# Attention probabilities transposed by VectorE in 32 by 32 blocks instead of by TensorE

## The chip, the cores and the metric

The kernel runs on one core of one Trainium2 chip. The metric is device time in microseconds (us) of one execution. The kernel before takes 2535.78 us, the median of 3 runs (2535.55 to 2538.28).

## The reference

One layer of a hybrid encoder in fp32 for 2048 tokens of 1024 features. The input projection gives, per token, 512 columns q and 128 columns each of k and v for a sliding-window attention (8 query heads and 2 key heads of 64), and 4 x 512 columns for a gated linear recurrence (HGRN2). The two outputs are put side by side, projected and added to the input; a cross attention into 256 memory tokens and a SwiGLU block follow. The part that the change touches is the sliding-window attention:

```python
s = jnp.einsum('bnqhgd,bnkhd->bnhgqk', qc, kband) * (Dh ** -0.5)
s = jnp.where(valid, s, NEG_INF)
p = jax.nn.softmax(jnp.concatenate([s, sink], axis=-1), axis=-1)[..., :L]
o = jnp.einsum('bnhgqk,bnkhd->bnqhgd', p, vband)
```

Scores `s` come with queries on the rows. The product with `v` sums over keys, so on the chip the probabilities `p` must be turned: keys on the partitions.

## The kernel before, in words

Every fp32 product is made of products of a high and a low half (`hi`, `lo`: the rounded value and what rounding left over), so TensorE does two or three matmuls for each.

**Stages.** (1) `in_first` makes the input projection of the first 1024 tokens (to about 275 us of the span). (2) A mixed stretch follows, to about 604 us: the attention `swa` for 16 tiles of 128 tokens ("pairs" n = 0 to 15, each with the tile before it as keys), the recurrence `hgrn` for tiles 0 to 7, and the input projection of the other 1024 tokens, `in_proj`, whose columns (`in_cols`, matmul lines L156 to L158) are dealt out between the pairs and give TensorE long runs of matmuls that wait for nothing of the attention. (3) The rest: tiles 8 to 15 of `hgrn`, the folding of the cross-attention weights, and then the large products (L1162 to L1164), which take about three quarters of the time.

**One pair.** `swa_front` loads q and k from DRAM (`z_d`) twice over both halves of the partitions, and makes the low halves on VectorE and ScalarE (L787, L788 for q, L1001, L1002 for k); TensorE makes the scores (L822, L823, into PSUM), VectorE masks them and takes the minimum (L827), ScalarE the exponential with its sum (L831), GpSimd adds the sink's share (L834, L837), VectorE takes the reciprocal and scales (L839, L842). `swa_back`, called one pair later, turns the probabilities on TensorE in squares of 128 (L856, 16 for each pair, 8 for the first), makes halves out of PSUM (L860 on ScalarE, L861 on VectorE), multiplies with v (L865, L866), adds the two halves (L869, L870) and stores 256 KB (`y_d<-ys`, L78).

**What sets the order.** The Tile framework's scheduler orders the instructions once, when the program is built; each engine then works off its own list in that order, and a waiting instruction holds up all that stand behind it on its engine. DMAs are issued by SyncE (SP), from one list too (L75 loads, L78 stores), a few by GpSimd. In the program's list each of SP's DMAs waits for one of eight semaphores in turn, which the DMA eight places ahead of it sets when it lands.

Of the kernel before, what the change touches and what calls it, by code (L numbers as in the profile page):

```python
# [48 lines left out]
class Layer:  # L49
# [111 lines left out]
    def run(self):  # L161
# [4 lines left out]
        self.z_d = tc.dram_tile([DIN, T], F32, name="z_d")  # L166

# [26 lines left out]
    def mix(self):  # L194
        tc, I = self.tc, self.I
        kw = dict(reuse_waits="tile")
        with contextlib.ExitStack() as left:
# [5 lines left out]
            with (  # L203
                tc.tile_pool(name="t1", bufs=3, **kw) as self.ts,
                tc.tile_pool(name="t2", bufs=3, **kw) as self.tb,
                tc.tile_pool(name="s1", bufs=2, side="right", **kw) as self.st_pool,
                contextlib.ExitStack() as at,
            ):
                self.banks(at, "ps1", **MOST)
                self.raws = 3  # L210
                u = self.in_first()
# [52 lines left out]
            with (  # L264
# [6 lines left out]
                self.raws = 4  # L271
# [164 lines left out]
    def pair_tile(self):  # L436
        self._n += 1
        return self.st_pool.tile([P, 2, D], F32, tag="pair", name=f"pair_{self._n}", bufs=5)
# [27 lines left out]
    def in_first(self):  # L466
# [154 lines left out]
        z = self.pair_tile()  # L621
        for s in range(2):
            for i in range(2):
# [3 lines left out]
                nc.scalar.activation(z[:, i, s * 512:(s + 1) * 512], ps, AF.Copy)  # L627
        for i in range(2):
            self.store(self.z_d[c0 + i * P:c0 + (i + 1) * P, TB:2 * TB], z[:, i, :])
        return u  # L630

    def in_block(self, ca, cb, x, ahead, beside, get, plain, between):
# [16 lines left out]
        def out(i, j, a, b):  # L649
            c0 = (ca, cb)[i] * P  # L650
            if plain:
                self._n += 1
                t = self.st_pool.tile([P, 512], F32, tag="part", name=f"zp_{self._n}", bufs=3)
                nc.scalar.activation(t, a, AF.Copy)
                self.store(self.z_d[c0:c0 + P, j * 512:(j + 1) * 512], t)
                return
            if not z:
                z.append(self.pair_tile())
            zs = z[0][:, i, j * 512:(j + 1) * 512]
# [10 lines left out]
            else:  # L670
                self._n += 1
                t = self.st_pool.tile([P, 512], F32, tag="part", name=f"th_{self._n}", bufs=3)
# [3 lines left out]
        def after():  # L676
# [14 lines left out]
            for i, c in enumerate(() if plain else (ca, cb)):  # L691
                self.store(self.z_d[c * P:(c + 1) * P, 0:TB], z[0][:, i, :])
# [16 lines left out]
    def in_cols(self, b, u, cols, e1):  # L709
# [5 lines left out]
        for s in range(TB // 512):  # L715
            sl = slice(s * 512, (s + 1) * 512)
            for i, c in enumerate(cols):
# [4 lines left out]
                if c0 < C_QH or C_IH <= c0 < C_GH:  # L722
# [11 lines left out]
        for i, c in enumerate(cols):  # L734
# [5 lines left out]
            self.store(self.z_d[c0:c0 + P, b * TB:(b + 1) * TB], z[i])  # L740
# [32 lines left out]
    def swa_front(self, n, kinds):  # L773
# [7 lines left out]
        for g in range(2):  # L781
            qd = ph.tile([P, 4, P], F32, tag="qd", name=f"qd{n}_{g}", bufs=2)
            qsrc = z[g * 256:(g + 1) * 256, t0:t0 + P].rearrange("(h d) t -> d h t", d=64)
# [3 lines left out]
            nc.scalar.activation(q, qd, AF.Copy, scale=-0.125)  # L787
            nc.vector.scalar_tensor_tensor(q[64:128], qd[64:128], -0.125, f32(q[64:128]), ALU.mult, ALU.subtract)  # L788
            qs.append(q)

        kr = ph.tile([P, 2, M], F32, tag="kr", name=f"kr{n}")
        kl = ph.tile([P, 2, M], F32R, tag="kl", name=f"kl{n}")
        kh = ph.tile([P, 2, M], F32R, tag="kh", name=f"kh{n}")
        o = M - nk * P
        ksrc = z[C_KA:C_VA, t0 + P - nk * P:t0 + P].rearrange("(g d) t -> d g t", d=64)
        self.load(kr[0:64, :, o:], ksrc)
        self.load(kr[64:128, :, o:], ksrc)
        self.split(kr[:, :, o:], kh[:, :, o:], kl[:, :, o:])
# [6 lines left out]
        nc.scalar.activation(vst[:, 0, 0:64], pv[:, 0:64], AF.Copy)  # L805
        nc.scalar.activation(vst[:, 1, 64:128], pv[:, 64:128], AF.Copy)
        nc.vector.tensor_tensor(vst[:, 0, 64:128], pv[:, 0:64], f32(vst[:, 0, 0:64]), ALU.subtract)
        nc.vector.tensor_tensor(vst[:, 1, 0:64], pv[:, 64:128], f32(vst[:, 1, 64:128]), ALU.subtract)
# [4 lines left out]
        for g in range(2):  # L813
            mn = self.small("w_mn", 4)
            den = self.small("w_den", 4)
            for i2 in range(2):
                s = ph.tile([P, 2, M], F32, tag="S", name=f"S{n}_{g}{i2}", bufs=6)
                S.append(s)
# [5 lines left out]
                for r in range(2):  # L824
# [3 lines left out]
                        out=s[:, r, o:], in0=ps[:, r * M + o:(r + 1) * M], in1=self.wmask[:, o:],  # L828
                        op0=ALU.add, op1=ALU.min, scale=1.0, scalar=self.nsink[:, h:h + 1],
                        accum_out=mn[:, i:i + 1])  # L830
                    nc.scalar.activation(s[:, r, o:], s[:, r, o:], AF.Exp, bias=mn[:, i:i + 1], scale=-1.0,  # L831
# [5 lines left out]
            nc.gpsimd.tensor_tensor(dn, den, se, ALU.add)  # L837
            rd = self.small("w_rd", 4)
            nc.vector.reciprocal(rd, dn)  # L839
            for i in range(4):  # L840
                a = S[2 * g + i // 2][:, i % 2, o:]
                nc.vector.tensor_scalar_mul(a, a, rd[:, i:i + 1])  # L842
        return S, vs

    def swa_back(self, n, kinds, S, vs):
        nc, ph = self.nc, self.sw
        nk = len(vs)
        o = M - nk * P
        kinds = itertools.cycle(kinds)
        ys = ph.tile([P, 4, P], F32, tag="ys", name=f"ys{n}")  # L850
        for g in range(2):
            t = []
            for kb in range(nk):
                ps = self.bank(next(kinds))
                for i in range(4):
                    nc.tensor.transpose(ps[:, i * P:(i + 1) * P],  # L856
                                        S[2 * g + i // 2][:, i % 2, o + kb * P:o + (kb + 1) * P], self.ident)
                th = ph.tile([P, 512], F32R, tag="pth", name=f"pth{n}_{g}{kb}", bufs=3)
                tl = ph.tile([P, 512], F32R, tag="ptl", name=f"ptl{n}_{g}{kb}", bufs=2)
# [967 lines left out]
```

## Time and profile before

The profiled execution has a span of 2530.8 us at a mean granted TensorE clock of 0.997; the median of the runs is 5.0 us longer than this span, which begins at the first and ends at the last instruction.

| part of the trace | us |
|---|---|
| span | 2530.8 |
| median of the runs, less span | 5.0 |
| TensorE busy over the span | 2496.8 (99%) |
| VectorE busy over the span | 1794.5 (71%) |
| stretch 270 to 604.8: TensorE busy | 330.02 of 334.80 |
| the same stretch: VectorE busy | 283.55 |
| the same stretch: ScalarE busy | 209.34 |
| last matmul of the in-projection in the stretch, start | 587.89 |
| last attention matmul (pair 15), start | 603.86 |

TensorE's durations overlap, since a matmul is recorded until its end while the next has begun; what a matmul costs TensorE is read from the distance of the starts of two that follow one another.

### The profile page before, as it was taken

The numbers are of one execution on the slowest core, as the hardware profiler recorded it, in microseconds if no ns is written. First come the engines' busy times: TensorE is split into PE (matmuls) and PEld (weight loads), VectorE is DVE, ScalarE is ACT, GpSimd is POOL, SyncE is SP. The second block draws the span as 40 slices with busy tenths as digits, with TensorE's granted clock in tenths as the row PEclk, the third lists the DMA queues.
The fourth block names the chain that finished last, engine by engine and source line by source line (L and its number), as shares of the span: only waits on it lengthen the run. The fifth ranks groups of instructions, "written<-read, shape, count | busy, mean of one in ns | idle before, by whom it ended". The sixth has DMA issues, their size and how long they took to land.

```text
span 2530.8 us, 34134 instructions
## 1 busy us (share of the span) xinstructions
PE 2496.8 (99%) x11942; PEld 2087.0 (82%) x11942; DVE 1794.5 (71%) x2863; ACT 1262.1 (50%) x2627; POOL 375.2 (15%) x540
## 2 busy tenths in 40 slices
PE   9999999999999999999999999999999999999998
PEld 8878888888987888878878888888888888888886
DVE  8785488986557889988866655576566557664766
ACT  5453466655565576566753333353333335443543
POOL 4231344321401111112200000000000000000022
PEclk9999999999999999999999999999999999999999
DMA  6455645673887996758944322254354334565776
GB/s 199 152 167 177 176 145 156 199 248 114 276 311 261 299 335 196 251 175 256 346 161 168 135 77 93 80 192 154 129 208 167 117 130 155 182 178 112 228 173 153
DMA packets 305133, 470.07 MB, mean 186 GB/s; under 512 B 21440, under 2 KB 193472, under 8 KB 304960
## 3 DMA queue, kind: packets, MB, share of 16 engines
q1 hardware_dynamic: 298912, 445.86, 52.7%
q0 software_dynamic: 6048, 22.02, 5.1%
q8 instruction: 94, 1.54, 0.3%
q14 instruction: 79, 0.65, 0.1%
HBM read 301.09 MB, written 166.72 MB: 185 GB/s over the span
## 4 chain that ended last, share of the span: by engine, by line
PE 84%; DVE 6%; DMA 4%; ACT 3%; issue 2%; POOL 1%; SPq 0%; DVEq 0%; POOLq 0%; ACTq 0%
PE psm L1164 23%; PE psm L1162 23%; PE psm L1163 22%; PE psg L156 2%; PE psg L158 2%; PE psg L157 2%; DVE T L1002 1%; DVE S L1002 1%; DMA raw<-in_wo_x_dram 1%; ACT junk L1533 1%; SPq L75 0%; DMA row<-h_d 0%; PE pss L156 0%; PE pss L157 0%; PE pss L158 0%
## 5 line engine op out<-in xcount | busy, mean ns | idle before, releaser
L1162 PE MATMUL psm<-T,S 128*128 128x512 f32 x2680 | 1034.3, 391 | 10.3 <-ACT part L1177 5.6
L1163 PE MATMUL psm<-T,S 128*128 128x512 f32 x2680 | 1042.9, 390 | 1.5 <-DVE T L1002 1.4
L1164 PE MATMUL psm<-T,S 128*128 128x512 f32 x2680 | 1029.8, 390 | 3.7 <-DVE S L1002 3.7
L1162 PEld LDWEIGHTS psm<-T,S 128*128 128x128 f32 x2680 | 503.2, 188 | 122.5 <-ACT part L1177 9.9
L1164 PEld LDWEIGHTS psm<-T,S 128*128 128x128 f32 x2680 | 503.4, 188 | 111.1 <-DVE S L1002 6.7
L1163 PEld LDWEIGHTS psm<-T,S 128*128 128x128 f32 x2680 | 503.5, 188 | 107.2 <-DVE T L1002 3.7
L999 ACT ACTIVATE S<-sum 128x512 fp32r<-128x512 f32 (+1 forms) x370 | 224.3, 620 | 375.7 <-PE psm L1164 274.2
L1002 DVE TENSOR_TENSOR S<-sraw,S 128x512 fp32r<-128x512 f32 (+1 forms) x315 | 212.1, 680 | 237.2 <-ACT S L999 234.1
L1177 ACT ACTIVATE part<-psm 128x512 f32<-128x512 f32 x285 | 168.8, 597 | 260.4 <-PE psm L1164 241.9
L1002 DVE TENSOR_TENSOR S<-sum,S 128x512 fp32r<-128x512 f32 (+1 forms) x388 | 258.5, 675 | 45.2 <-ACT S L999 41.2
L999 ACT ACTIVATE S<-sraw 128x512 fp32r<-128x512 f32 (+1 forms) x300 | 184.4, 618 | 109.2 <-PE psm L1164 107.3
L1566 POOL DMA_DIRECT2D y_d<-row x16 | 14.1, 879 | 1077.0 <-DVE row L1748 1026.1
L1002 DVE TENSOR_TENSOR T<-row,T 128x1024 fp32r<-128x1024 f32 (+1 forms) x112 | 131.0, 1186 | 27.7 <-ACT T L999 25.7
L156 PE MATMUL psg<-u,whi 128*128 128x512 f32 x320 | 127.6, 399 | 1.3 <-DVE z L730 1.3
L158 PE MATMUL psg<-u,wlo 128*128 128x512 f32 x320 | 127.4, 399 | 0.0
L157 PE MATMUL psg<-u,whi 128*128 128x512 f32 x320 | 127.4, 398 | 0.0
L1533 ACT ACTIVATE junk<-row 128x512 f32<-128x512 f32 x160 | 99.7, 625 | 43.5 <-DVE row L1555 21.2
L999 ACT ACTIVATE T<-row 128x1024 fp32r<-128x1024 f32 (+1 forms) x112 | 113.4, 1032 | 7.3 <-DMA row<-in_w_down_dram 2.8
L1699 DVE TENSOR_TENSOR row<-psm,part 128x512 f32<-128x512 f32 x66 | 44.1, 688 | 71.3 <-PE psm L1164 71.3
L1002 DVE TENSOR_TENSOR wlo<-raw,whi 128x1024 fp32r<-128x1024 f32 x52 | 64.0, 1232 | 41.4 <-ACT whi L999 30.6
L1748 DVE TENSOR_TENSOR row<-psm,part 128x512 f32<-128x512 f32 x72 | 49.2, 689 | 49.3 <-PE psm L1164 49.1
L831 ACT ACTIVATE S<-S,w_mn 128x256 f32<-128x256 f32 (+1 forms) x128 | 63.1, 496 | 41.4 <-DVE w_mn L827 41.0
(355 smaller groups left out, 3541.3 us busy)
## 6 DMA issues: line engine op xcount, KB each, us to landing
sraw<-in_w_gate_dram SPq DMA_DIRECT2D x44, 512.0 KB, 3.8
sraw<-in_w_up_dram SPq DMA_DIRECT2D x44, 512.0 KB, 3.7
hid_d<-row SPq DMA_DIRECT2D x44, 512.0 KB, 2.7
sraw<-hid_d SPq DMA_DIRECT2D x32, 512.0 KB, 4.4
sraw<-in_w_in_dram SPq DMA_DIRECT2D x48, 256.0 KB, 3.8
z_d<-pair SPq DMA_DIRECT2D x20, 512.0 KB, 3.3
raw<-in_w_in_dram SPq DMA_DIRECT2D x20, 512.0 KB, 4.6
z_d<-z SPq DMA_DIRECT2D x20, 512.0 KB, 3.8
```

Source lines behind the costliest of these rows:

```text
L156: nc.tensor.matmul(ps, ah, bh, start=(i == 0), stop=False)
L157: nc.tensor.matmul(ps, ah, bl, start=False, stop=False)
L158: nc.tensor.matmul(ps, al, bh, start=False, stop=(i == n - 1))
L831: nc.scalar.activation(s[:, r, o:], s[:, r, o:], AF.Exp, bias=mn[:, i:i + 1], scale=-1.0, accum_out=den[:, i:i + 1])
L999: self.nc.scalar.activation(hi, raw, AF.Copy)
L1002: self.nc.vector.tensor_tensor(lo, raw, f32(hi), ALU.subtract)
L1162: nc.tensor.matmul(ps, s[:, 0, k, :], t[:, 0, k, :], start=st, stop=False, **kw)
L1163: nc.tensor.matmul(ps, s[:, 0, k, :], t[:, 1, k, :], start=False, stop=False, **kw)
L1164: nc.tensor.matmul(ps, s[:, 1, k, :], t[:, 0, k, :], start=False, stop=sp, **kw)
L1177: nc.scalar.activation(t, ps, AF.Copy)
L1533: self.nc.scalar.activation(junk, a, AF.Square, scale=float(D) ** -0.5, accum_out=to)
L1748: nc.vector.tensor_tensor(d, a, b, ALU.add)
```

## The change

- **Turning.** A new function `swa_turn` scales the probabilities, turns them with four VectorE transposes of 128 x 512 (L888), each of which turns all its 32 x 32 blocks in place of the grid, into a tile `pb` (one buffer), and puts the blocks in their places with 16 DMAs from `pb` to an operand tile `pt` (two buffers), 32 partitions by 512 values each (64 KB in runs of 2 KB). It is called after the `swa_back` of the pair before.
- **Back.** `swa_back` does no TensorE transposes. It makes the halves out of `pt` (L906 on ScalarE, L907 on VectorE in place) for the matmuls L908 and L909. The two halves of the result are no more added on VectorE: one ScalarE copy per head group, a store of one half by SP, and an adding DMA of the other by GpSimd, which waits until the store has landed.
- **q and k.** The input projection stores q (scaled by -0.125) and k as high and low halves to `zq_d` and `zk_d` (one ScalarE copy and one VectorE operation per 128 x 512, `halves`; two stores instead of one), and `swa_front` loads the halves where they are used. L787, L788 and the k halves L1001, L1002 of `swa_front` are gone. v's halves take one operation each instead of two.
- **Buffers.** `pair` 5 to 6, `part` 3 to 5 in the first stage, `S` two tiles of 4 heads instead of six of 2.

```diff
+    def halves(self, c0, src, hi, lo):
+        f = -0.125 if c0 < C_KA else 1.0
+        self.nc.scalar.activation(hi.bitcast(F32R), src, AF.Copy, scale=f)
+        self.nc.vector.scalar_tensor_tensor(lo.bitcast(F32R), src, f, hi, ALU.mult, ALU.subtract)
+    def store_halves(self, c0, t0, *parts):
+        dst, r = (self.zq_d, c0) if c0 < C_KA else (self.zk_d, c0 - C_KA)
+        for e, t in enumerate(parts):
+            self.store(dst[e, r:r + P, t0:t0 + t.shape[1]], t)
...
-            qd = ph.tile([P, 4, P], F32, tag="qd", name=f"qd{n}_{g}", bufs=2)
-            self.load(qd[0:64], qsrc)
-            self.load(qd[64:128], qsrc)
             q = ph.tile([P, 4, P], F32R, tag="qs", name=f"qs{n}_{g}", bufs=2)
-            nc.scalar.activation(q, qd, AF.Copy, scale=-0.125)
-            nc.vector.scalar_tensor_tensor(q[64:128], qd[64:128], -0.125, f32(q[64:128]), ALU.mult, ALU.subtract)
+            for e in range(2):
+                self.load(f32(q[64 * e:64 * e + 64]),
+                          self.zq_d[e, g * 256:(g + 1) * 256, t0:t0 + P].rearrange("(h d) t -> d h t", d=64))
...
+    def swa_turn(self, n, S, nk):
+        t = ph.tile([P, 4, 2, 2, P], F32, tag="pb", name=f"pb{n}")
+        for g, (s, dn) in enumerate(S):
             rd = self.small("w_rd", 4)
             nc.vector.reciprocal(rd, dn)
             for i in range(4):
+                nc.vector.tensor_scalar_mul(s[:, i, o:], s[:, i, o:], rd[:, i:i + 1])
+            for k in range(2 - nk, 2):
+                nc.vector.transpose(t[:, :, g, k].rearrange("p b (h j) -> p b h j", h=4),
+                                    s[:, :, k * P:(k + 1) * P].rearrange("p h (b i) -> p b h i", b=4))
+        d = ph.tile([P, 4, 2, 2, P], F32R, tag="pt", name=f"pt{n}", bufs=2)
+        for a in range(4):
+            for b in range(4):
+                self.load(f32(d[b * 32:(b + 1) * 32, a, :, 2 - nk:]), t[a * 32:(a + 1) * 32, b, :, 2 - nk:])
+        return d
...
-                for i in range(4):
-                    nc.tensor.transpose(ps[:, i * P:(i + 1) * P],
-                                        S[2 * g + i // 2][:, i % 2, o + kb * P:o + (kb + 1) * P], self.ident)
-                nc.scalar.activation(th, ps, AF.Copy)
-                nc.vector.tensor_tensor(tl, ps, f32(th), ALU.subtract)
+                lo = pt[:, :, g, 2 - nk + kb]
+                hi = ph.tile([P, 4, P], F32R, tag="pth", name=f"pth{n}_{g}{kb}", bufs=3)
+                nc.scalar.activation(hi, f32(lo), AF.Copy)
+                nc.vector.tensor_tensor(lo, f32(lo), f32(hi), ALU.subtract)
...
-            nc.scalar.activation(ys[a], pr[c], AF.Copy)
-            nc.vector.tensor_tensor(ys[a], pr[a], ys[a], ALU.add)
-        self.store(self.y_d[n, :, 0:512], ys.rearrange("p k t -> p (k t)"))
+        dst = self.y_d[n, :, 0:512].rearrange("(g d) c -> d g c", g=2)
+        self.store(dst, ys[0:64])
+        nc.gpsimd.dma_start(dst, ys[64:128], accum_op=ALU.add)
```

The scheduler's order moves with it. First, **TensorE around the last matmul of the in-projection in the mixed stretch** (`psg`, L158). `pth13_11` and `ptl13_11` are halves of pair 13's probabilities, `kh15`, `kl15` and `qs15` keys and queries of pair 15. Before:

```order
L157 MATMUL psg_876_6451<-u1_11_2217,whi_873_6419 128x512
L158 MATMUL psg_876_6451<-u1_11_2217,wlo_873_6420 128x512
L866 MATMUL psh_832_6081<-ptl13_10_6069,vst12_5542 128x512
L865 MATMUL psh_832_6081<-pth13_11_6077,vst13_5754 128x512
L866 MATMUL psh_832_6081<-ptl13_11_6078,vst13_5754 128x512
L822 MATMUL pss_849_6217<-kh15_6167,qs15_1_6162 128x256
```

After the change (`vr13` is pair 13's v, `kk13` its keys):

```order
L157 MATMUL psg_826_6239<-u1_11_2247,whi_823_6207 128x512
L158 MATMUL psg_826_6239<-u1_11_2247,wlo_823_6208 128x512
L945 MATMUL psg_827_6274<-qq8_6269,k18_6267 128x192 x2
L908 MATMUL pss_739_5469<-pth11_00_5470,vst10_5023 128x512
L841 MATMUL pss_750_5606<-ident_80,vr13_5604 128x128
L908 MATMUL pst_740_5481<-pth11_10_5482,vst10_5023 128x512
L909 MATMUL pss_739_5469<-pt11_5319,vst10_5023 128x512
L908 MATMUL pss_739_5469<-pth11_01_5475,vst11_5220 128x512
L909 MATMUL pss_739_5469<-pt11_5319,vst11_5220 128x512
L858 MATMUL pst_753_5614<-kk13_5601,qs13_0_5595 128x256
```

Before, the rest of pair 13, most of pair 15's scores and the backs of pairs 14 and 15 stand behind that matmul; after, the whole backs of pairs 11 to 15 and the fronts of pairs 13 to 15 do. The matmuls of stage 3 follow behind both.

Second, **VectorE behind the last in-projection result** (`z_824`, L770), after the change; `pb12` is the turned tile of pair 12, `S13_0` pair 13's scores:

```order
L770 SCALAR_TENSOR_TENSOR z_824_6211<-z_824_6211,psg_826_6239 128x512
L888 STREAM_TRANSPOSE pb12_5495<-S12_0_5418 128x4x128 x2
L888 STREAM_TRANSPOSE pb12_5495<-S12_1_5444 128x4x128 x2
L907 TENSOR_TENSOR pt11_5319<-pt11_5319,pth11_00_5470 128x4x128
L907 TENSOR_TENSOR pt11_5319<-pt11_5319,pth11_01_5475 128x4x128
L907 TENSOR_TENSOR pt11_5319<-pt11_5319,pth11_10_5482 128x4x128
L907 TENSOR_TENSOR pt11_5319<-pt11_5319,pth11_11_5487 128x4x128
L863 ISA S13_0_5613,w_mn_751_5611<-pst_753_5614,wmask_2400,nsink_551 128x256
```

The same steps then follow for pairs 13, 14 and 15, with nothing of another job between them.

Third, **SP in the same place**, after the change; before, there were no transfers between tiles on this list:

```order
L75 DMA pt11_5319<-pb11_5302 32x512 x7
L78 DMA y_d_60<-ys10_5275 64x2x512
L75 DMA pt11_5319<-pb11_5302 32x512 x9
L75 DMA qs13_0_5595<-zq_d_58 64x4x128 x2
L75 DMA qs13_1_5598<-zq_d_58 64x4x128 x2
L75 DMA kk13_5601<-zk_d_59 64x4x256 x2
L75 DMA pt12_5512<-pb12_5495 32x512 x10
L78 DMA y_d_60<-ys11_5468 64x2x512
L75 DMA pt12_5512<-pb12_5495 32x512 x6
```

The loads of pair 13's q and k stand behind the last nine transfers of pair 11, and the store of pair 11's result stands between the transfers of pair 12. Between the first q load and the last store of the attention SP's list holds 229 DMAs before and 488 after, 256 of them transfers to `pt`.

More of the change, by code (lines that the diff above doesn't have):

```diff
@@ L651, in out @@
             if plain:
[L652 to L655, printed above, removed]
+                t = []
+                for e in range(2 if c0 < C_VA else 1):
+                    self._n += 1
+                    t.append(self.st_pool.tile([P, 512], F32, tag="part", name=f"zp_{self._n}", bufs=self.parts))
+                if c0 < C_VA:
+                    self.halves(c0, a, *t)
+                    self.store_halves(c0, j * 512, *t)
+                else:
+                    nc.scalar.activation(t[0], a, AF.Copy)
+                    self.store(self.z_d[c0:c0 + P, j * 512:(j + 1) * 512], t[0])
                 return
@@ L721, in in_cols @@
                 zs = z[i][:, sl]
[L722 removed]
+                if c0 < C_VA:
+                    if s == 0:
+                        low = self.io_tile("u")
+                    self.halves(c0, ps, zs, low[:, sl])
+                elif c0 < C_QH or C_IH <= c0 < C_GH:
                     nc.scalar.activation(zs, ps, AF.Copy)
@@ L739, in in_cols @@
                     pass
-            self.store(self.z_d[c0:c0 + P, b * TB:(b + 1) * TB], z[i])
+            if c0 < C_VA:
+                self.store_halves(c0, b * TB, z[i], low)
+            else:
+                self.store(self.z_d[c0:c0 + P, b * TB:(b + 1) * TB], z[i])
         return e1
```

99 lines of the change are left out of this document (54 added, 45 removed).

## The prediction

> **What bounds the kernel now.** I read the page first, then the stretch that the change touches by windows, then the end of that stretch instruction by instruction.
>
> ```profile
> PE 2496.8 (99%) x11942; PEld 2087.0 (82%) x11942; DVE 1794.5 (71%) x2863; ACT 1262.1 (50%) x2627; POOL 375.2 (15%) x540
> ...
> 300.00:330.00 30.00, 30.00 (x174) 26.14 (x173) 22.30 (x62) 16.80 (x54) 8.07 (x15) 1.00 0.44 134
> ...
> 570.00:600.00 30.00, 28.28 (x147) 23.22 (x146) 26.83 (x77) 20.28 (x61) 4.29 (x10) 0.94 0.36 120
> ...
> 270.00:604.80 334.80, 330.02 (x1850) 283.31 (x1849) 283.55 (x694) 209.34 (x611) 114.71 (x176) 0.99 0.55 176
> ```
>
> The windows' columns are TensorE, its weight loads, VectorE, ScalarE, GpSimd, clock, DMA share, GB/s. TensorE sets the time almost everywhere, in the mixed stretch too: 330.0 of 334.8 us. But VectorE is at 85% there, against 71% over the span, and only the last window loses TensorE time and clock (28.28 us, 0.94). The timeline of TensorE shows why:
>
> ```profile
> 587.66 0.39 PE L157 MATMUL psg<-u,whi 128*128 128x512 f32 x1
> 587.89 0.40 PE L158 MATMUL psg<-u,wlo 128*128 128x512 f32 x1
> 588.12 0.39 PE L866 MATMUL psh<-ptl,vst 128*128 128x512 f32 x1
> ...
> 588.82 0.28 PE L822 MATMUL pss<-kh,qs 128*128 128x256 f32 x1
> 588.93 0.28 PE L823 MATMUL pss<-kl,qs 128*128 128x256 f32 x1
> ...
> 592.85 0.51 PE L865 MATMUL psh<-pth,vst 128*128 128x512 f32 x1 [0.80 <-DVE ys L870]
> 594.12 0.65 PE L856 MATMUL pss<-ident,S 128*128 128x128 f32 x4 [0.77 <-DVE w_mn L827]
> ...
> 596.09 0.63 PE L865 MATMUL psh<-pth,vst 128*128 128x512 f32 x1
> 596.52 0.63 PE L866 MATMUL psh<-ptl,vst 128*128 128x512 f32 x1
> ...
> 600.31 0.27 PE L856 MATMUL pss<-ident,S 128*128 128x128 f32 x1
> 600.42 0.27 PE L856 MATMUL pst<-ident,S 128*128 128x128 f32 x1
> ...
> 603.86 0.48 PE L866 MATMUL psh<-ptl,vst 128*128 128x512 f32 x1
> 604.17 0.60 PE L918 MATMUL pst<-ident,v 128*128 128x128 f32 x4
> ```
>
> As long as in-projection matmuls (L156 to L158) are left, TensorE has work that waits for no softmax. At 588.1 us they are used up; then come stalls, and matmuls 0.43 us apart (596.09, 596.52) instead of 0.23. This bare tail lasts 16 us, until 604.2.
>
> **What the change takes from TensorE.**
>
> ```profile
> L856 PE MATMUL pst<-ident,S 128*128 128x128 f32 x120 | 21.5, 277 | 0.2 <-DVE w_mn L827 0.2
> L856 PE MATMUL pss<-ident,S 128*128 128x128 f32 x128 | 21.5, 277 | 0.8 <-DVE w_mn L827 0.8
> ```
>
> 248 transposes go. The records overlap; their distance is 0.11 us (600.31, 600.42), so TensorE saves 248 x 0.11 = 27.3 us. Were it bound by its own work throughout, the time would be 2535.8 - 27.3 = 2508.5 us.
>
> Whether it can be had depends on the bare tail. By the order, 216 transposes (8 for pair 0, 16 each for 1 to 13) stood ahead of the last in-projection matmul: 23.8 us less. Attention work has moved behind it as well: 21 matmuls of the backs 11 to 13 (0.23 us each, 4.8 us) and 36 of the fronts 13 to 15 (0.12 us by 588.82 and 588.93, 4.3 us), with three small ones. The cover so ends 33 us earlier, at about 554.9, and from there the pairs 12 to 15 must come through alone. What follows in stage 3 is the same work as before. **So the change in time is the shift of the tail's end against 604.2.**
>
> **VectorE's work per pair in that tail.**
>
> ```profile
> 39.52 1.31 DVE L1431 STREAM_TRANSPOSE pair<-pair 128x512 f32<-128x512 f32 x2
> 40.75 2.73 DVE L1002 TENSOR_TENSOR u<-pair,u 128x512 fp32r<-128x512 f32 x4
> ...
> 591.19 0.48 DVE L827 CUSTOM_DVE_ANT_0 S<-psh,wmask,nsink 128x256 f32<-128x256 f32 x1
> ...
> 591.59 0.48 DVE L827 CUSTOM_DVE_ANT_0 S<-psh,wmask,nsink 128x256 f32<-128x256 f32 x1
> ...
> 594.79 0.69 DVE L861 TENSOR_TENSOR ptl<-pss,pth 128x512 fp32r<-128x512 f32 x1
> 595.39 0.68 DVE L861 TENSOR_TENSOR ptl<-pst,pth 128x512 fp32r<-128x512 f32 x1
> 595.99 0.17 DVE L839 RECIPROCAL w_rd<-w_dn 128x4 f32<-128x4 f32 x1
> ...
> 599.11 1.13 DVE L842 TENSOR_SCALAR S<-S,w_rd 128x256 f32<-128x256 f32 x4
> 600.15 0.68 DVE L861 TENSOR_TENSOR ptl<-pss,pth 128x512 fp32r<-128x512 f32 x1
> ```
>
> From start to start: a 128 x 512 block transpose 0.6 us ((40.75 - 39.52) / 2), four are 2.4; L907 like L861, 0.6, four are 2.4; a masked minimum 0.40, eight are 3.2; eight scalings 8 x 0.26 = 2.1; reciprocals and v's half 0.5. Sum 10.6 us per pair. On VectorE as a whole the four new transposes replace q's, k's and the result's operations:
>
> ```profile
> L788 DVE SCALAR_TENSOR_TENSOR qs<-qd,qs 64x512 fp32r<-64x512 f32 x32 | 25.8, 809 | 21.1 <-ACT qs L787 20.2
> L1002 DVE TENSOR_TENSOR kl<-kr,kh 128x512 fp32r<-128x512 f32 x15 | 10.5, 700 | 1.9 <-POOL kh L1001 1.7
> ```
>
> **The round trip.** The new link in each pair's chain is 16 DMAs of 64 KB, which SP issues one by one. Nothing in this trace moves from SBUF to SBUF; the nearest row is the 128 KB store of block-transposed tiles (smallest, median and largest issue in ns):
>
> ```profile
> L78 SPq DMA_DIRECT2D un_d<-pair x32: 318/457/950, 40.9 to 168.7; - x32
> ...
> DMA to landing us min/median/max: 2.0/2.3/12.2
> ```
>
> Issuing is 16 x 0.318 = 5.1 to 16 x 0.457 = 7.3 us, then 2.0 to 2.3 us until the last has landed: 7.1 to 9.6 us. `pb` has one buffer, so the next pair's transposes wait for all of it: at least 2.4 + 7.1 = 9.5, likely 12.0 us per pair.
> A rule of the Trainium skill speaks for less (DMA: Bandwidth & Descriptors, "Issuing engines are not separate DMA queues"): the time to initiate a DMA on a sequencer is usually small relative to the DMA itself. By it a round trip would be little over one landing, VectorE's 10.6 us would hide it, and the tail would be rival B's; the row above disagrees here, 7.3 us of issuing against 2.3 of landing.
>
> **Two waits more.** The store of the previous pair's result stands amid the 16 transfers, and GpSimd's adding DMA waits for it to land, with the next pair's softmax sums queued behind it:
>
> ```profile
> y_d<-ys SPq DMA_DIRECT2D x16, 256.0 KB, 3.9
> L1566 POOL DMA_DIRECT2D y_d<-row x16 | 14.1, 879 | 1077.0 <-DVE row L1748 1026.1
> L837 POOL TENSOR_TENSOR w_dn<-w_den,w_se 128x4 f32<-128x4 f32 x32 | 10.5, 329 | 20.2 <-ACT w_se L835 19.9
> ```
>
> From one pair's transposes to the next by this way: 2.4, ten issues 4.6, the store's own 0.3, its landing 3.9, GpSimd's issue 0.9 and sum 0.3, reciprocal and four scalings 1.3: 13.7 us. The period is the longest of the three ways, between 10.6 and 13.7; I take 13, as the last two are near each other and the loads of the next pair's q and k stand behind them on SP.
>
> **The sum.** Last in-projection result on VectorE at 554.9 + 1.3 = 556.2. Three periods of 13 to pair 15's transposes, 39; these 2.4; a bare round trip 9.6; then 0.6 for the first high half on ScalarE, 2.4 for four L907 and 0.5 for the last matmuls, 3.5. The tail ends at 610.7, 6.5 us later than 604.2. With 10.6 and 7.1 it is 601.0 (3.2 sooner; B below goes a little lower), with 13.7, 9.6 and matmuls at half pace (18 us of them, a third bare, 3 us) 616 (12 later). The profiled execution lies 5.0 us under the median: 2530.8 + 6.5 + 5.0 = 2542.3, and 1 us for the first stage below: **2543 us**.
>
> **The first stage.** 12 halves are added on VectorE (0.68 each, 8.2 us) and as many stores, where q and k are projected.
>
> ```profile
> 0.00:60.00 60.00, 56.27 (x341) 49.92 (x342) 48.79 (x63) 34.13 (x61) 30.02 (x45) 1.00 0.65 200
> ...
> 120.00:180.00 60.00, 57.10 (x249) 46.31 (x248) 56.46 (x75) 37.49 (x58) 27.25 (x32) 1.00 0.49 155
> ```
>
> VectorE has 3.5 to 11 us free in each of these 60 us, so TensorE's 57 cover most: 0 to 8.2, I take 1. In the second half the eight halves lie behind the in-projection.
>
> **Rivals.** (B) *The round trips hide*: VectorE is the bound. Behind 556.2 its order holds 16 transposes (9.6), 20 L907 (12.0), 24 minima (9.6), 24 scalings (6.2) and small ones (1.1): 38.5 us; with what the last trip leaves bare, 7.1 - 2.4 for L907 of pair 14, and 0.5 for the last matmuls the tail ends at 599.9, 4.3 sooner, and the time is 2531.5, give or take 3. For it: VectorE's 10.6 a pair is within 1.4 of the likely trip. Against: `pb` has one buffer, and the store's way takes 13.7. (C) *SP becomes the bound in the whole stretch.* Its list there grows from 229 to 488 DMAs, and each waits for the one eight places before it. From 275 to 600 us, 325 us, this allows a mean of 8 x 325 / 488 = 5.3 us from issue to landing. The rows are
>
> ```profile
> qd<-z_d SPq DMA_DIRECT2D x64, 128.0 KB, 2.9
> raw<-in_w_in_dram SPq DMA_DIRECT2D x20, 512.0 KB, 4.6
> SPq L75 <- DMA y_d<-sg: 33.4, 14, 4.6
> ```
>
> so below it on the mean, but the third, a wait, shows the rotation biting already. Beyond 5.3 it decides; at 5.8 the stretch ends at 275 + 354 = 629, 25 later: 2561 us. (D) *The full gain*: the pairs run so far ahead of the in-projection that no bare tail comes; 2508.5. For it: a pair's 10.6 to 13.7 us is less than the 20 us that a pair has on the mean in the stretch (325 / 16). Against it stands the order, which puts five backs behind the cover. By the rows the same 128 x 128 square costs TensorE 0.11 us and VectorE 0.6 / 4 = 0.15, so 37 us of transposes are what D would have to hide on VectorE. The Trainium skill, too, would leave them where they were (VectorE: DVE Perf Modes, "Rules for kernel authors": transpose 128 x 128 on TensorE if a PSUM destination will do).
>
> **Chances.** Forecast (bare tail at the trips' pace) 0.52, B 0.20, C 0.16, D 0.09, something else 0.03. The forecast's own range is 2532 to 2549. About 0.2% (5 us: under 2530.7, over 2540.9) is what a measurement can tell from no change. Faster: D, half of B and a little of the rest, 0.20. Same: the other half of B and a quarter of the forecast, 0.23. Slower: what is left, 0.57. The range leaves out D and the worse half of C: 2524 to 2562.
>
> **What would show it.** Right: TensorE idle in gaps between L908 groups from about 555 to 610, waiting for L907, with its clock under 1.0 there; L888 waiting for DMAs `pt<-pb`, 12 to 14 us apart for pairs 13 to 15; no idle TensorE before. B: those L888 wait for nothing. C: SP waiting for DMA landings through the stretch, q and k late, TensorE idle at each pair from 300 on. D: no TensorE gap over 1 us from 555 to the last L909, at about 577 (604.2 - 27.3). The forecast is wrong if the stretch ends before 601, if the L888 of the last pairs are under 11 us apart, or if the first 275 us grow by over 5.

## The result and the profile after

The changed kernel takes 2612.25 us (median of 4 runs, 2609.62 to 2615.66) against 2535.66 us: 1.031 times the time before, 95% interval 1.0295 to 1.0320. That is 76.6 us slower, where 7 were forecast and the range ended at 26 above. The profiled execution has a span of 2613.9 us, 83.1 longer than before; all but 1.2 of that lies ahead of the last attention matmul at 685.8 us, since the rest of the span is nearly as long as it was (2613.9 - 685.8 = 1928.1, before 2530.8 - 603.9 = 1926.9).

The chain of work that ended last, on the page of the kernel before (shares of the span; SPq is SP's issuing):

```profile
PE 84%; DVE 6%; DMA 4%; ACT 3%; issue 2%; POOL 1%; SPq 0%; DVEq 0%; POOLq 0%; ACTq 0%
```

The page of the changed kernel: busy times, two of the rows over 40 slices, and the same chain.

```profile
PE 2498.8 (96%) x11694; PEld 2075.9 (79%) x11694; DVE 1787.8 (68%) x2849; ACT 1243.2 (48%) x2582; POOL 360.6 (14%) x540
...
PE   9999999885699999999999999999999999999998
...
PEclk9999999986799999999999999999999999999999
...
PE 71%; DMA 10%; DVE 7%; SPq 5%; ACT 3%; issue 3%; POOL 2%; DVEq 0%; POOLq 0%; ACTq 0%
```

248 matmuls fewer, as counted; TensorE's busy sum is no smaller, since its matmuls are recorded longer where the clock is low, in the slices from 523 to 719 us (128x512: 0.39 us in the line at 593.86 below, 0.79 and 0.44 in those behind it). SP and the DMAs have come into the chain. The timeline of TensorE gives the three times that matter, and its windows the rest:

```profile
283.78 0.30 PE L858 MATMUL pst<-kk,qs 128*128 128x128 f32 x1 [0.58 <-DMA kk<-zk_d]
...
593.86 0.39 PE L158 MATMUL psg<-u,wlo 128*128 128x512 f32 x1
598.21 1.65 PE L945 MATMUL psg<-qq,k 128*128 128x192 f32 x4 [3.97 <-DVE z L770]
606.64 0.79 PE L908 MATMUL pss<-pth,vst 128*128 128x512 f32 x1 [6.79 <-ACT pth L906]
...
685.77 0.44 PE L909 MATMUL pst<-pt,vst 128*128 128x512 f32 x1
```

```profile
300.00:450.00 150.00, 143.05 (x771) 122.70 (x770) 116.63 (x273) 86.28 (x254) 55.09 (x87) 0.99 0.75 201
450.00:594.00 144.00, 124.97 (x602) 102.56 (x600) 93.83 (x221) 60.75 (x182) 31.23 (x54) 0.94 0.87 255
594.00:686.00 92.00, 37.07 (x113) 25.56 (x112) 48.72 (x141) 34.91 (x102) 11.23 (x25) 0.57 0.59 152
```

The attention begins 8.5 us later than before (283.8 for 275.3). The in-projection's cover ends at 593.9, not at 554.9: 8.5 from the first stage, and most of the other 30 from TensorE standing still inside the mixed stretch (by the windows it is idle 7 us of the first 150 and 19 of the next 144). The bare tail then takes 91.9 us, not 55.8. So 39 + 36 us came on top of the forecast's 610.7. What TensorE, ScalarE, GpSimd and VectorE waited for (microseconds in all, times, longest):

```profile
PE pss L908 <- ACT pth L906: 49.5, 8, 11.4
ACT pth L906 <- DMA pt<-pb: 50.0, 13, 9.9
PE pst L858 <- DMA kk<-zk_d: 7.0, 6, 2.8
POOL y_d L914 <- DMA y_d<-ys: 48.5, 10, 17.3
DVE pb L888 <- DMA pt<-pb: 15.1, 6, 4.2
```

The operand tile's transfers are late. Their rows (smallest, median and largest issue in ns, then issue to landing in us), and SP's timeline in the tail:

```profile
L75 SPq DMA_DIRECT2D pt<-pb x256: 507/589/1803, 295.1 to 677.4; - x128
...
DMA to landing us min/median/max: 1.8/2.3/8.4
```

```profile
598.13 6.05 SPq L75 DMA_DIRECT2D pt<-pb  x9
604.28 2.62 SPq L75 DMA_DIRECT2D qs<-zq_d  x4
606.94 1.27 SPq L75 DMA_DIRECT2D kk<-zk_d  x2
608.43 6.26 SPq L75 DMA_DIRECT2D pt<-pb  x10
617.23 0.64 SPq L78 DMA_DIRECT2D y_d<-ys  x1
617.90 3.83 SPq L75 DMA_DIRECT2D pt<-pb  x6
621.84 2.91 SPq L75 DMA_DIRECT2D qs<-zq_d  x4
624.79 1.34 SPq L75 DMA_DIRECT2D kk<-zk_d  x2
626.23 5.63 SPq L75 DMA_DIRECT2D pt<-pb  x9
```

SP is at work nearly without a break from 598 to 632, save for one wait from 614.7 to 617.2 for pair 11's result, with six transfers of pair 12 behind it. Summed over its rows from 275 us to the last attention matmul, SP spends 111 us on issuing 219 DMAs before and 306 us on 487 DMAs after, 160 of them on the 256 transfers (0.62 us each on the mean): 34% of the stretch, then 74%. For the landing of an earlier DMA, the eight-semaphore rotation included, SP waits 26 us there before and 40 after (its waits on DMAs summed), and the mean time to landing of all its DMAs is 4.2 us.

### The profile page after: what moved, and what is told of

It is laid out like the page before. It is cut to its first block, busy times and chain, and to the rows that moved or that the text cites. A ratio compares the mean times of both kernels' runs of the same rounds, so it can differ in the third digit from the quotient of the medians.

```text
span 2613.9 us, 33884 instructions
## 1 busy us (share of the span) xinstructions
PE 2498.8 (96%) x11694; PEld 2075.9 (79%) x11694; DVE 1787.8 (68%) x2849; ACT 1243.2 (48%) x2582; POOL 360.6 (14%) x540
## 4 chain that ended last, share of the span: by engine, by line
PE 71%; DMA 10%; DVE 7%; SPq 5%; ACT 3%; issue 3%; POOL 2%; DVEq 0%; POOLq 0%; ACTq 0%
PE psm L1207 21%; PE psm L1209 21%; PE psm L1208 21%; SPq L75 4%; DMA pt<-pb 1%; DVE S L1047 1%; DVE T L1047 1%; DVE pb L888 1%; DMA pair<-in_x_dram 1%; DMA row<-in_w_down_dram 1%; ACT junk L1578 1%; DMA y_d<-ys 0%; DMA qs<-zq_d 0%; DMA kk<-zk_d 0%; PE pss L156 0%
## 5 line engine op out<-in xcount | busy, mean ns | idle before, releaser
L158 PE MATMUL psg<-u,wlo 128*128 128x512 f32 x320 | 127.5, 399 | 0.0
```

The lines of the kernel that those rows point to most:

```text
L158: nc.tensor.matmul(ps, al, bh, start=False, stop=(i == n - 1))
```

## The experiments

Three theories. **S**: SP is bound by the number of DMAs it must issue, and what is queued behind them (q, k, the next pair's transfers) comes late. **D**: the way from scaling to operand tile is too long for the place that the order gives a pair's back. **L**: the bytes of the transfers, or **G**: GpSimd's adding DMA, are at fault. Every edit makes the scheduler order anew; the last section of experiments shows that this alone can move the time by 13 us, so a smaller difference below is no proof of one cause. The kernel before, run beside these on the same chip, took 2533.4 to 2536.6 us at the median. Most of the slower kernels were run twice.

**Fewer bytes, same count.** Edit (the operand tiles are set to zero once):

```diff
-                self.load(f32(d[b * 32:(b + 1) * 32, a, :, 2 - nk:]), t[a * 32:(a + 1) * 32, b, :, 2 - nk:])
+                self.load(f32(d[b * 32:(b + 1) * 32, a, 1, 1]), t[a * 32:(a + 1) * 32, b, 1, 1])
```

> The change, but each of the 16 transfers of a pair carries only one of its four runs of 512 bytes (16 KB instead of 64 KB; the rest of the operand tile stays zero, so the attention part of the output is left wrong). The count of transfers and SP's list stay. Theory S (SP issues the transfers one by one, 256 x 0.62 us, and q and k of the next pairs queue behind them): nothing but the landing gets shorter, 2590 to 2615 us. Theory L (bytes: the DMA engines are 80 to 90% busy in the stretch and the transfers land late): 3/4 of the bytes gone, 2540 to 2565 us. Theory G (GpSimd's adding DMA holds up the softmax sums): unchanged, 2612.

Measured: 2594.4 us (before 2536.6). The rows of the transfers:

```profile
L75 SPq DMA_DIRECT2D pts<-pb x256: 507/589/1658, 296.2 to 674.1; - x128
```

Issuing 16 KB takes SP as long as issuing 64 KB, 0.589 us. A quarter of the bytes won 18 us of 77, and the time lies in S's range: L is not the main cause.

**Fewer transfers.** Edit (operand tiles as in the last):

```diff
         for a in range(4):
-            for b in range(4):
-                self.load(f32(d[b * 32:(b + 1) * 32, a, :, 2 - nk:]), t[a * 32:(a + 1) * 32, b, :, 2 - nk:])
+            self.load(f32(d[a * 32:(a + 1) * 32, a, :, 2 - nk:]), t[a * 32:(a + 1) * 32, a, :, 2 - nk:])
```

> The change, but only 4 of a pair's 16 transfers, of full size (the other blocks of the operand tile stay zero, output wrong there). As many bytes as in the run with 16 small ones, a quarter of the issues. S: SP saves 192 x 0.62 = 119 us, the tail's period falls from 17 to about 11 us and the stretch no longer starves: 2530 to 2550 us. L: the same as the run with 16 small transfers. G: 2600 to 2612.

Measured: 2562.9 us, 49 us less than the change and 31 less than with as many bytes in 16 transfers, which were of 32 partitions each too. The count matters, as S says, but the time is above S's range: 26 us over before are left with SP issuing 175 us.

**No adding DMA.** Edit:

```diff
-            nc.scalar.activation(ys[:, g, :]..., ps..., AF.Copy)
-        self.store(dst, ys[0:64])
-        nc.gpsimd.dma_start(dst, ys[64:128], accum_op=ALU.add)
+            nc.scalar.activation(yr, pr[c], AF.Copy)
+            nc.vector.tensor_tensor(yr, pr[a], yr, ALU.add)
+        self.store(self.y_d[n, :, 0:512], ys)
```

> The change, with the result's halves added as before (a ScalarE copy and a VectorE addition for each head group, one store of 256 KB, no adding DMA by GpSimd). G: the 48.5 us that GpSimd's adding DMAs wait fall out of the softmax chain, 2560 to 2590 us. S: only SP's store gets cheaper (16 x 0.3 = 5 us) while VectorE gets 22 us of additions: 2600 to 2620. L: 2600 to 2612.

Measured: 2601.5 us, 11 less, which a new order alone could do. G's 48.5 us of waiting on GpSimd were mostly not on the path.

**The halves of q and k alone.** Edit: the change, with `swa_back`'s TensorE transposes of the kernel before and its way of adding the result.

> Only the other half of the change: q and k stored and loaded as halves, v's halves in one operation each; probabilities turned by TensorE in 128 x 128 squares, halves out of PSUM and the result added and stored as before (S in four tiles of four heads). S, L and G all put the loss on what is taken out here: 2530 to 2540 us, VectorE with about 20 us less in the mixed stretch, first stage within 2 us. If the halves themselves cost the time (extra stores, VectorE in the first stage), over 2550.

Measured: 2532.4 us (before 2536.6; 10 runs against 13), ratio 0.9986, interval 0.9977 to 0.9996. So the loss lies in the turning by VectorE and its transfers, and this half of the change is worth some 3.5 us, less than the 5 us that count as a difference here. It is the fastest version of this study.

**Half of the issues on ScalarE.** Edit:

```diff
-                self.load(f32(d[b * 32:...]), t[a * 32:...])
+                (self.nc.scalar if b % 2 else self.nc.sync).dma_start(f32(d[b * 32:...]), t[a * 32:...])
```

> The change, with every second of a pair's 16 transfers issued by ScalarE instead of SP. Theory S (the issues on one list): a pair's transfers are issued in about 5 us instead of 10, and SP's list loses 80 us in the stretch; if ScalarE's own work (62% busy there before) takes the 8 issues at the 0.6 us of SP, 2565 to 2590 us. If only the depth of the chain counts (two pairs in flight, TensorE's list has the scores of pair n+2 behind the back of pair n), the saving of 5 us per two pairs: 2575 to 2595. If ScalarE's softmax is held up by issues that wait for the turned tile, slower than the change: over 2615.

Measured: 2596.8 us, 15 less, and above the ranges that S (2565 to 2590) and the chain's depth (2575 to 2595) gave. ScalarE pays as much for an issue as SP:

```profile
L893 ACTq DMA_DIRECT2D pt<-pb x128: 513/602/1578, 295.7 to 654.0; - x128
```

128 of them are 81 us of ScalarE's list, which also waits there for the turned tile; SP's sum falls to 218 us. The issues were moved to an engine that sits in the same chain; that this is why so little was won is not shown.

**Through DRAM in six DMAs.** Edit, in place of the 16 transfers:

```diff
+        for a in range(4):
+            self.store(self.pb_d[n, :, :, a, :].rearrange("b i x -> i b x"), t[a * 32:(a + 1) * 32]...)
+        for h in range(2):
+            self.load(f32(d[:, 2 * h:2 * h + 2])..., self.pb_d[n, :, :, 2 * h:2 * h + 2, :].rearrange("b i a x -> (b i) a x"))
```

> The change, but the blocks are put in place by way of DRAM: 4 stores of 256 KB and 2 loads of 512 KB for a pair instead of 16 transfers of 64 KB (pair 0 as before). S (count of issues): SP issues some 3.5 us instead of 10 for each pair, its sum in the stretch falls from 310 to about 210 us, near the run with a quarter of the transfers: 2555 to 2580 us. L (bytes, busy DMA engines): twice the bytes, slower than the change, 2620 to 2660. Depth of the chain alone: way of 2.4 + 2.3 + 0.7 + 6 = 11.4 us instead of 14.8 seen in the tail, so 1.7 us less per pair, 2585 to 2600.

Measured: 2611.9 us, as slow as the change, though SP issues only 222 us. No forecast was met. Two landings now stand in a row (medians 4.9 and 6.7 us in the list of DMA issues), and twice the bytes move; these are what can have taken back what the shorter list gives, and the run doesn't tell them apart. A short list alone is not enough.

**Five pairs only.** Edit, on top of the halves alone: `swa_turn` and the back of the change for pairs 1, 3, 5, 7 and 9, TensorE transposes for the others.

> The kernel with q and k stored as halves and TensorE transposes, but pairs 1, 3, 5, 7 and 9 turned by VectorE with 16 transfers each, as in the change (result added as before in all; pt and pth with one buffer less). TensorE loses 80 transposes, 8.8 us, all of them well ahead of the bare tail; SP's list gets 80 more DMAs, 48 us of its some 200 free us. If SP's count and the tail were all that spoilt the change: 2520 to 2528 us. If each turned pair stalls TensorE by itself (a pair's way of 15 us is longer than what the pairs around it cover): 2540 to 2560.

Measured: 2544.5 us, ratio 1.0048 (1.0034 to 1.0062), 12 us slower than the halves alone and in the range of pairs that stall TensorE by themselves, nearly all of it in the stretch (the attention starts at 282.5 and ends at 613.8; with the halves alone 283.0 and 603.6). The 8.8 us of TensorE were not had even far from the tail; how much of the loss is the pairs' own and how much another order was not told apart.

**Back two pairs later.** Edit:

```diff
-        for n in itertools.chain(pairs, (None,)):
+        for n in itertools.chain(pairs, (None, None)):
...
-            if last is not None:
-                self.swa_back(*last)
+            if len(late) == 2 or n is None and late:
+                self.swa_back(*late.pop(0))
             if n is not None:
-                last = n, kinds(n), self.swa_turn(n, S, len(vs)), vs
+                late.append((n, kinds(n), self.swa_turn(n, S, len(vs)), vs))
```

> The change, with the back of a pair two pairs behind its front instead of one (v's halves in 4 buffers, the high halves pth in 2). Nothing is added or taken away on any engine or on SP. On TensorE's list the matmuls worth 29 to 55 us stand between a pair's scores and its back for pairs 0 to 11 (before this edit 20 to 34), and in-projection matmuls stand up to the end of the last pair. Theory D (the way through scaling, transposes, SP and landing takes longer than what the scheduler put between scores and back, and TensorE's list then stands still): most of the loss goes, 2520 to 2560 us. Theory S (SP's 310 us of issuing are themselves too much for the stretch): 2580 to 2612, since SP issues just as much.

Measured: 2592.1 us, 20 less than the change and far from the 2520 to 2560 of D. TensorE now hardly waits for operand tiles (`PE pss L908 <- ACT pth L906` 4.3 us in one wait), but:

```profile
PE pst L858 <- DMA kk<-zk_d: 37.3, 7, 21.3
```

Scores wait for keys, whose load stands on SP's list behind the transfers. The longest of these waits, 21.3 us up to 624.8, shows it on SP's timeline: the second half of the keys is issued behind 16 transfers.

```profile
609.99 0.61 SPq L75 DMA_DIRECT2D kk<-zk_d  x1
610.70 10.16 SPq L75 DMA_DIRECT2D pt<-pb  x16
620.91 0.63 SPq L75 DMA_DIRECT2D kk<-zk_d  x1
```

The wait has only moved; this speaks for S.

**Transfers that nobody reads.** Edit (pt in one buffer):

```diff
-        return d
+        return t
...
-                nc.vector.tensor_tensor(lo, f32(lo), f32(hi), ALU.subtract)
+                src, lo = lo, ph.tile([P, 4, P], F32R, tag="ptl", ..., bufs=2)
+                nc.vector.tensor_tensor(lo, src, f32(hi), ALU.subtract)
```

> The change, with all transfers still issued but read by nobody: ScalarE and VectorE make the halves straight from the turned tile pb, so blocks are not in their places (output wrong); low halves into two small buffers, pt in one buffer. VectorE's next transposes still wait until the transfers out of pb have landed. D: the way gets some 15 us shorter, the cover that the list has (12 to 35 us) is enough: 2520 to 2550. S: SP's 310 us of issuing stay, q and k still queue behind the transfers: 2575 to 2612.

Measured: 2587.2 us (two runs, 2582.4 and 2591.9), 25 less than the change. With no operand waiting for the transfers two thirds of the loss stay, in S's range. One wait for them is left, that of VectorE's next transposes for `pb` (8.9 us in five waits).

**No transfers.** Edit: as the last, without the 16 loads.

> As the run in which nobody reads the transfers, but with the transfers taken out (output wrong: blocks not in their places). All work of TensorE, VectorE and ScalarE of the change is there. If VectorE's and ScalarE's work and TensorE's list allow the gain of 27 us at all: 2508 to 2515 us. If VectorE (93% of the shortened stretch) is a bound by itself: 2525 to 2545.

Measured: 2539.3 us, ratio 1.0013 (1.0003 to 1.0024): another 48 us less. But TensorE's 27 us don't appear here either. With the result added as before, so that GpSimd waits for nothing:

> The change without its transfers (halves made straight from the turned tile, blocks not in their places) and with the result's halves added and stored as before instead of by GpSimd's adding DMA. With the adding DMA this was 2539. If the adding DMA held up the softmax sums and the splits behind it on GpSimd there: 2510 to 2525 us, most of the 27 us of TensorE. If VectorE's order is what is left: 2535 to 2545, since it gets 22 us of additions back.

Measured: 2533.2 us, ratio 0.9989 (0.9980 to 0.9999). That lies between the two ranges, below the one for VectorE's order. Nothing but the engines' own work is left of the change, and it is worth 2.4 us. The windows of this kernel tell where the 27 us are:

```profile
300.00:450.00 150.00, 149.39 (x836) 129.10 (x835) 139.70 (x337) 103.27 (x306) 60.72 (x91) 1.00 0.63 184
450.00:570.00 120.00, 116.77 (x575) 97.05 (x574) 104.34 (x243) 62.34 (x173) 34.94 (x51) 0.99 0.77 248
570.00:600.00 30.00, 16.87 (x63) 11.55 (x61) 27.30 (x80) 18.40 (x54) 3.16 (x8) 0.73 0.32 96
```

TensorE is full up to 570; then the cover is used up and VectorE (27.3 of 30) sets the pace of the last pairs, with TensorE at 16.87 us and 0.73 of its clock. That is the bare tail, with VectorE alone.

**The same transfers on a kernel without the change's chain.** Edit: the halves alone, plus for pairs 1 to 15

```diff
+            for a in range(4):
+                for b in range(4):
+                    self.load(d[b * 32:(b + 1) * 32, a], S[b // 2][0][a * 32:(a + 1) * 32, b % 2 * 2:b % 2 * 2 + 2, :]...)
```

> The kernel with q and k stored as halves and TensorE transposes (2532 us), with the change's 16 transfers of 64 KB added for each of the pairs 1 to 15, from the scaled probabilities into a tile that nobody reads. No step of the attention waits for them; they only stand on SP's list. S (SP's list is the bound: 240 more issues of 0.6 us, 150 us, and what queues behind them): SP's issuing rises from 126 to about 280 us, q and k come late, 2565 to 2595 us. D (the way from the transposes to the operand tile is what costs): no more than 2532 to 2545.

Measured: 2574.8 us (before 2535.6), 42 us over the halves alone, though no instruction reads the tile. SP issues 272 us. And the same bytes in 4 transfers of 128 partitions, `self.load(d[:, b], S[b // 2][0][:, ...])`:

> The kernel with halves and TensorE transposes, with as many bytes moved for nobody as in the run with 16 transfers for each pair (2574.8 us), but in 4 transfers of 128 partitions and 256 KB. Count of issues (S): 60 issues, not over 0.6 us each, 36 us on SP: 2532 to 2542. Bytes (L): as the run with 16, 2565 to 2580.

Measured: 2533.8 us, ratio 0.9998 (0.9988 to 1.0009). The rows of both:

```profile
L75 SPq DMA_DIRECT2D pt<-S x240: 507/588/1902, 305.4 to 653.0; - x120
```

```profile
L75 SPq DMA_DIRECT2D pt<-S x60: 464/542/1348, 305.2 to 590.7; - x60
```

1 MB for each pair costs nothing in 60 issues and 42 us in 240. The DMA engines' busy share (the last column but one) doesn't tell the two runs apart, and TensorE's busy time (the first column behind the comma) does; 16 transfers, then 4:

```profile
500.00:600.00 100.00, 89.66 (x436) 73.83 (x435) 61.80 (x154) 41.53 (x118) 17.89 (x32) 0.95 0.83 251
```

```profile
500.00:600.00 100.00, 99.21 (x523) 83.66 (x523) 77.32 (x202) 53.15 (x150) 17.05 (x35) 1.00 0.86 290
```

This settles S against L: what costs is the number of issues, at a median of 0.54 to 0.59 us each whether they carry 16, 64 or 256 KB. The wait for the semaphore of the DMA eight places ahead goes by the count too, but it is small: up to the last attention matmul SP waits for landings 38 us with 240 transfers, 31 with 60 and 32 without any.

**Three remedies together.** Edit: back two pairs later, half of the issues on ScalarE, no adding DMA.

> The change with three edits together: back two pairs behind the front, every second transfer issued by ScalarE, result's halves added as before without the adding DMA. Alone they won 20, 15 and 11 us. If they relieve separate waits: 2612 - 46 = 2566 us, still slower than before. If they relieve the same one (SP's list): 2580 to 2592. If ScalarE's issues and VectorE's additions now bind: over 2592.

Measured: 2601.1 us, slower than two of the three alone and in the range for ScalarE's issues and VectorE's additions. They don't add up; whether these two are the bound, or another order is, was not tested.

**The first stage.** It is 7.7 us longer with the halves alone too (the attention starts at 283.0). First, `halves` in that stage only where `C_KA <= c0 < C_VA` (k), and L787, L788 of the kernel before for q of pairs 0 to 7:

> The kernel with halves and TensorE transposes, but q of the first 1024 tokens is stored and split as before (L787, L788 of the kernel before, for pairs 0 to 7); q of the others and all of k stay halves. Theory F (the halves' VectorE work and stores hold up the first stage: the attention starts at 283.0 us of the span instead of 275.3, and the 11 us won later show as 3.5 only): eight of the first stage's added operations go, the attention starts at 276 to 279, 2525 to 2529 us. If the first stage is late for another reason (more part buffers, another order): 2531 to 2536.

Measured: 2547.0 us, ratio 1.0046; the attention starts at 286.3. With less added work the first stage is longer, so F's forecast fails; as the order is another one too, this doesn't show that the added work costs nothing. Next the buffers: the kernel before with pair 6 and part 5, and the halves with pair 5 and part 3.

> The kernel before with only the change's buffer counts (pair 6 instead of 5, part 5 instead of 3 in the first stage). If the buffers make another order and that order holds up the first stage: the attention starts at 280 us of the span or later, 2538 to 2545. If the halves' own work there does: starts at 275 to 276, 2533 to 2537.

> The kernel with halves and TensorE transposes, with the buffer counts of the kernel before (pair 5, part 3). If the buffers were what held up the first stage (the wait of 4 us at 109.8 behind a late load of x): the attention starts at 275 to 278, 2525 to 2529 us. If the halves' own tiles and work hold it up: at 283 or later, 2532 to 2542.

Measured: 2546.7 us, ratio 1.0046 (1.0029 to 1.0063), attention from 288.9; and 2538.1 us, ratio 1.0017 (1.0007 to 1.0026), from 285.8. The kernel before, with one buffer more here and two there and not one operation changed, loses 13 us, and in its profile the attention starts 13.5 later. So another order by itself can cost what the change lost in its first stage. But with the buffer counts of the kernel before the halves still start 10.5 us late, where their own work was forecast to hold up the stage: in each of the four runs the attention starts 8 to 14 us later than in the kernel before, and how much of the change's 8.5 is the halves' work, and how much the order, these runs don't tell. In the halves alone one wait shows how an order loses time:

```profile
104.81 1.06 ACT L446 ACTIVATE pair<-pair 128x1024 f32<-128x1024 f32 x1 [4.07 <-DMA pair<-in_x_dram]
...
114.23 0.53 PE L1246 MATMUL psm<-T,S 128*128 128x512 f32 x1 [4.01 <-ACT part L1261]
```

ScalarE stands behind a load of x, which was issued at 97.7; the copies that free PSUM banks stand behind it, and TensorE 4 us behind those. Which rule of the scheduler puts that load there was not found.

## Why the prediction was wrong

- **Direction right, mechanism of the tail right in part.** The tail after the last in-projection matmul is bare, and TensorE waits there for L906's and L907's operands at a low clock (0.57). Pairs 12 to 15 are turned at 605.91, 623.54, 641.37 and 663.24; pairs 12 and 15 waited for `pt<-pb` just before (3.2 and 4.2 us), pair 13 for nothing, and pair 14 by the profile for a load of v (5.1), two of its four transposes following only at 648.1.
- **The step that failed first: "issuing is 16 x 0.318 to 16 x 0.457".** It was 16 x 0.62 = 10.0 us, and behind it on the same list come the six loads of the next q and k (0.66 each, 3.9) and the store (0.7): 14.6 us of SP for each pair, more than the whole period of 13. The measured period is 17.6 to 21.9. The prediction read the price from `un_d<-pair`, whose form is another; the trace of before had nearer rows, which it didn't use, loads of 64 partitions at 0.62 each:

```profile
281.51 1.24 SPq L75 DMA_DIRECT2D qd<-z_d  x2
...
391.15 1.23 SPq L75 DMA_DIRECT2D qd<-z_d  x2
```

The tail's 36 us over the forecast are 10.7 until pair 12's transposes (pair 11's transfers are still being issued), 18.3 in the three periods and 7.0 behind pair 15's transposes. With the measured issue and store (10.0 and 0.7) in the prediction's own sum the period is 15.7 and the tail about 67 us (an estimate from these rows); the other 25 up to 91.9 are waits that the sum doesn't have, and which of them decide was not tested.

- **The second: "the cover ends at about 554.9".** It took TensorE to run without new stalls in the stretch, and SP's list there was costed only in rival C. The cover ended 39 us later. C, with SP as the bound in the whole stretch (chance 0.16), was the mechanism, but its bound was wrong: it counted eight DMAs in flight and a mean landing of 5.3 us as the limit. The mean was 4.2, below it, and the transfers' median 2.3; what decided was the issuing itself, 306 us on a list whose stretch took 329 us before, beside the waits that stand on the same list. So its 2561 us came out 51 too low.
- **Round trip or list?** The prediction's tail saw a chain through SP and put nothing on the list in the stretch; the runs show that the list costs more. With no operand waiting for the transfers they cost 42 us (on the halves alone) and 48 us (between the runs with and without transfers); reading them, the chain, cost 25 more.
- **GpSimd's wait** (way of 13.7 us): there, but small: taking the adding DMA out won 11 us with the transfers and 6 without (2539.3 to 2533.2), both less than a new order can do.
- **The first stage: put at 1 us, measured 8.5.** The 0 to 8.2 us were for VectorE's added work; that buffer counts and with them the scheduler's order can cost 13.5 had no term. Which of the two it was stays open.
- **Rival B's price was right for a kernel that doesn't exist.** Without transfers and adding DMA the tail ends at 607.6 with the attention 8 us late, 599.6 against B's 599.9, and the time is 2533.2 against 2531.5. Such nearness is in part luck: B counted 4.7 us for a last trip, which this kernel doesn't have, and left out the result's additions on VectorE, which it has; and the 8 us of the late start are made up for by a rest of the span that is 4 us shorter and runs that lie 3.0 over the profiled span and not 5.0. But VectorE alone would have eaten the 27 us of TensorE.
- **The Trainium skill's rule** (DMA: Bandwidth & Descriptors, "Issuing engines are not separate DMA queues"), that initiating a DMA is usually small relative to the DMA, holds for one of these at the most (0.589 us of issuing against 2.3 us to landing) and not for a pair's sixteen (10 us against 2.3). Its other half, that several issuing engines save the sequencer's time only, is not at odds with the run that shared the issues: SP's sum fell by 88 us, the time by 15.

## What to carry to other kernels

Before a step is moved off a full engine into DMAs, add up the issues on the queue that will carry them, with the duration of the row whose shape is nearest, and compare the sum with the stretch: here 0.6 us each made 160 us out of 256 small transfers, and 240 such that nobody read cost 42 us where the same bytes in 60 large ones cost nothing. Work that covers other work shrinks when it gets faster: even without the transfers the 27 us taken from TensorE were waited for at the end of the stretch, there for VectorE. And in a kernel whose order a scheduler makes, an edit without any cost of its own can move the time by 13 us, so a small gain is read only from the edit alone, and with that in mind.

## What the runs showed of the hardware

The issue of a transfer from SBUF to SBUF took SP a median of 0.589 us at 16 KB and at 64 KB (32 partitions), 0.542 us at 256 KB (128 partitions), and ScalarE 0.602 us at 64 KB. Landing took 2.1 us (16 KB), 2.0 to 2.3 us (64 KB) and 5.3 us (256 KB) at the median. That issuing hardly depends on the bytes at these sizes, and that a store's row of 0.457 us for 128 KB was no guide to it, had not been expected.
